# Softmax bias written by the masked score reduction, value halves split out of PSUM, first query stores on GpSimd's queue, and two steps placed later, in a hybrid mLSTM and window-attention layer

## The chip, the core and the metric

The kernel runs on one core of one Trainium2 chip. A core has TensorE (PE, matmuls), VectorE (DVE), ScalarE (ACT), GpSimd (POOL) and SyncE (SP, which here only issues DMAs); each works through its own queue in order, and semaphores tie the queues together. The metric is the device time of one execution in microseconds, and a kernel's time is the median of several runs.

## What is computed

One layer over 4096 tokens of width 1024, all in float32. The rows are normalised, projected to 3856 columns, and the columns feed two groups:

```
scores = (q @ k.T) * 64 ** -0.5                        # 8 query heads, 2 key/value heads, blocks of 128
scores = where(|i - j| <= 128, scores + bias, -1e30)   # T5 relative bias
m      = maximum(max(scores), sink)                    # one learned sink logit per head
p      = exp(scores - m)
out    = (p @ v) / (sum(p) + exp(sink - m))            # group B
h      = mLSTM(q, k, v, gates), forward + backward     # group A, chunks of 128, 4 heads of 128
y      = concat(groupnorm(sigmoid(o) * h) * silu(z_a), out * silu(z_b))
result = rmsnorm(x + y @ w_out)
```

## The kernel before

Four stages follow each other, and TensorE's order is the order of the code (`manual_schedule` for PE). The other engines' orders are made by a scheduler that simulates the program; `behind(c, ins)` tells it not to place an instruction ahead of `ins`, and `high_priority` lets it go ahead of others.

**Stage 1, `pass1` (about 0 to 606 us): window attention.** It runs over 16 blocks of 256 tokens. The fill work is projections with float32 split in two parts, high and low (`kproj`, `vproj`, `qproj`); between its matmuls lie the pieces of attention, four slots per block. A slot is a pair of a 128-token chunk and a key/value head. For slot `sl`, `att_a(sl + 2, g)` makes the scores of query group g = 0 to 3 two slots ahead (L380), adds the bias and reduces a row maximum on VectorE, straight from PSUM (L383, an instruction followed by a short one that reads out the accumulator). The four maxima lie in the tile `st`; after the fourth, L390 forms `NG = min(-max, -sink)` for all four, and four activations (L392) take `exp(s + NG)`. `att_t(sl, i)` transposes 128 columns of four score tiles into a PSUM buffer `tp` of the tag "b", which has two buffers (L412), and ScalarE and VectorE split it into `pt` (L414, L415): the second of these frees the buffer. `att_o(sl - 1, i)` multiplies with the values (L426); ScalarE's copy L438 and VectorE's add L439 empty its result `op` (tag "c", one buffer) into `ab`, which SP stores (L441).

Once per block, `norm_rows(b + 4, LAST["act"])` squares two row tiles on ScalarE (L213, `jk`), behind the latest exponential. `vproj` gathers both halves of a value tile from the PSUM tile `vp` into `vg` in SBUF (L523, L524; 144 columns, 128 of values and 16 of gates), and L527 and L528 split `vg` into `vt`. GpSimd works beside all this on row scaling (L265), splits (L275) and sums (L690 to L693). `sinks()` (L395) closes the stage, and `rnorm` (L798) takes the reciprocal of the row sums `R`, [128, 256], on VectorE (L800).

**Stage 2, `pass2` (about 606 to 1210 us): keys, queries and values of the mLSTM.** It runs over 8 blocks of 512 tokens, from b = 7 down to 0. `qkproj` makes projections, convolution taps (L1053) and SiLU (L1057, L1058) and stores the result to DRAM on SP's queue (L1060). For b = 7 the operands are still in SBUF; the operands `xb` of b = 6 come through SP's queue (L868, eight loads). `ktp` transposes keys into the PSUM tag "b" and splits them (L1101, L1102). `weigh(n)` multiplies a value tile with gate weights (`wvr`, one direction on GpSimd and one on VectorE, L1112) and splits it (L1114, L1115), and `kvmm` multiplies keys with it and carries the state C (L1137), storing kf and C on GpSimd's queue (L1143, L1128). At b = 0 the fill is that of the next stage (L1342).

Stages 3 and 4 (`pass3`, `tail`) scan the chunks and project the output; the change doesn't touch them.

Of the kernel before, what the change touches and what calls it, by code (L numbers as in the profile page):

```python
# [9 lines left out]
F32 = mybir.dt.float32  # L10
F32R = mybir.dt.float32r
BF16 = mybir.dt.bfloat16
AF = mybir.ActivationFunctionType
ALU = mybir.AluOpType
# [10 lines left out]
EV = 400  # L25
# [3 lines left out]
def f32(ap):  # L29
    return ap.bitcast(F32)  # L30
# [85 lines left out]
def behind(c, ins):  # L116
    return c.tc.issue_after(ins.ins) if ins is not None else ExitStack()
# [43 lines left out]
def pass1(c):  # L161
    nc, tc, A = c.nc, c.tc, c.A
    NB = 16
    with ExitStack() as es:
# [168 lines left out]
        bias = []  # L333
# [27 lines left out]
        def att_a(sl, g):  # L361
# [10 lines left out]
            if g == 0:  # L372
                st = wk.tile([128, 4], F32, tag="st", bufs=4, name=f"st{sl}")
                ST[sl] = ([], list(range(jl // 128, jr // 128)), st)
            ps, _, mx = ST[sl]
            ng, rs = c.NG[:, kv, n, :], c.R[:, n, kv, :]
            sp = c.ps("a", [128, 384], f"sp{sl}_{g}")
            qt = qb[kv * 2 + m][:, qc // 64 + half].rearrange("p z q -> p (z q)")
            for z in range(2):
# [4 lines left out]
                                           in1=bias[0][:, kv * 2 + m, lo - 64 * half:hi - 64 * half],  # L384
                                           op0=ALU.add, op1=ALU.max, scale=1.0, scalar=-3e38,
                                           accum_out=mx[:, g:g + 1])
            ps.append(s)
            if g < 3:
                return
            nc.vector.scalar_tensor_tensor(ng, mx, -1.0, nsink[:, kv].rearrange("p h m -> p (h m)"), ALU.mult, ALU.min)  # L390
            for g in range(4):
                LAST["act"] = nc.scalar.activation(ps[g][:, kept(g)], ps[g][:, kept(g)], AF.Exp, bias=ng[:, g:g + 1],  # L392
                                                   accum_out=rs[:, g:g + 1])
# [11 lines left out]
        def att_t(sl, i):  # L405
            ps, js, _ = ST[sl]
            if i >= len(js):
                return
            j = js[i]
            tp = c.ps("b", [128, 512], f"tp{sl}_{j}")  # L410
            for g in range(4):
                nc.tensor.transpose(tp[:, g * 128:(g + 1) * 128], ps[g][:, j * 128:(j + 1) * 128], c.ident)  # L412
            pt = PT[sl, i] = xtile(c, [128, 2, 512], F32R, f"pt{sl}_{j}")
            nc.scalar.copy(pt[:, 0, :], tp)  # L414
            nc.vector.tensor_sub(pt[:, 1, :], tp, f32(pt[:, 0, :]))  # L415
# [90 lines left out]
        def vproj(b):  # L506
            R = {}

            def unit(i, k):
# [12 lines left out]
                with tc.high_priority(offset=EV):  # L522
                    nc.scalar.copy(vg, vp[:, 1, :])  # L523
                    nc.vector.tensor_add(vg, vp[:, 0, :], vg)  # L524
                vt = wk.tile([128, 2, 128], F32R, tag="v", bufs=7, name=f"v{n}")
                vv = vg[:, 0:128].rearrange("p (a d) -> p a d", a=2)
                nc.scalar.copy(vt[:, :, 0:64], vv)  # L527
                nc.vector.tensor_sub(vt[:, :, 64:128], vv, f32(vt[:, :, 0:64]))  # L528
                V[n] = vt
# [153 lines left out]
        fill = qproj(NB - 2) + kproj(NB - 1) + vproj(NB - 1) + qproj(NB - 1) + v2_units(range(31, 27, -1))  # L683
        interleave(fill, pieces)
        sinks()

# [111 lines left out]
def rnorm(c):  # L798
    nc = c.nc
    nc.vector.reciprocal(c.R, c.R)  # L800
    tp = c.ps("b", [128, 2, 128], "rtp")
# [76 lines left out]
def pass2(c):  # L878
    nc, tc, A = c.nc, c.tc, c.A
    with ExitStack() as es:  # L880
# [138 lines left out]
        def qkproj(b, m):  # L1019
# [6 lines left out]
            def unit(lo, hi, k, j):  # L1026
# [28 lines left out]
                def finish():  # L1055
# [3 lines left out]
                    dst = c.k_d if m >= 4 else c.q_d  # L1059
                    nc.sync.dma_start(dst[4 * b:4 * b + 4, :, h * 128:h * 128 + 128].rearrange("n p t -> p n t"),  # L1060
                                      acc.rearrange("p (n t) -> p n t", n=4))
# [83 lines left out]
        for b in range(7, -1, -1):  # L1145
# [40 lines left out]
            def kvp(n, hh):  # L1186
                if hh == 0 and n > n3 - 3:
                    weigh(n - 1)
                kvmm(n, hh)
# [735 lines left out]
```

## Time and profile before

| what | us |
|---|---|
| three runs | 2173.66, 2176.89, 2175.59 |
| median | 2175.59 |
| the profiled execution, its own time | 2170.39 |
| its span, first to last instruction | 2168.7 |
| TensorE busy | 2116.4 |
| VectorE, ScalarE, GpSimd busy | 1547.1, 1132.2, 704.2 |

The profile is of one execution. Its groups give, for a line of the code, the engine, the operation, the output and input tiles, the number of instructions, busy time and mean duration, and the idle time in front of them with what ended it. The table of waits adds such idle time up by who waited for whom: total, number of waits, longest. The timeline lists instructions by start and duration. A TensorE that is busy nearly all the time makes its idle stretches the part that other engines can give back.

### The profile page before, as it was taken

The numbers are of one execution on the slowest core, as the hardware profiler recorded it, in microseconds if no ns is written. First come the engines' busy times: TensorE is split into PE (matmuls) and PEld (weight loads), VectorE is DVE, ScalarE is ACT, GpSimd is POOL, SyncE is SP. The second block draws the span as 40 slices with busy tenths as digits, with TensorE's granted clock in tenths as the row PEclk, the third lists the DMA queues.
The fourth block names the chain that finished last, engine by engine and source line by source line (L and its number), as shares of the span: only waits on it lengthen the run. The fifth ranks groups of instructions, "written<-read, shape, count | busy, mean of one in ns | idle before, by whom it ended". The sixth has DMA issues, their size and how long they took to land. (4 is left out here: it accounts for less than half of the span.)

```text
span 2168.7 us, 35317 instructions
## 1 busy us (share of the span) xinstructions
PE 2116.4 (98%) x12034; PEld 1834.4 (85%) x12034; DVE 1547.1 (71%) x3259; ACT 1132.2 (52%) x2764; POOL 704.2 (32%) x1049
## 2 busy tenths in 40 slices
PE   8999999999999999999999999999999999999998
PEld 7999999999887887888887888888888788888886
DVE  6777777878876786667566777777777443777776
ACT  7778777778654444444433455555555321323323
POOL 3575666653014234322310322223222111112222
PEclk9999999999999999999999999999999999999999
DMA  8563544433228556743676988888888998667775
GB/s 269 181 208 135 194 142 187 161 139 113 64 91 263 188 170 217 246 159 112 216 223 239 340 272 273 254 265 278 268 273 290 353 359 279 181 178 187 192 196 144
DMA packets 286432, 460.71 MB, mean 212 GB/s; under 512 B 23851, under 2 KB 151851, under 8 KB 284716
## 3 DMA queue, kind: packets, MB, share of 16 engines
q1 hardware_dynamic: 246880, 323.94, 46.5%
q0 software_dynamic: 39136, 134.25, 19.0%
q8 instruction: 95, 1.56, 0.3%
q14 instruction: 85, 0.70, 0.1%
q10 hardware_dynamic: 236, 0.27, 0.0%
HBM read 305.20 MB, written 153.17 MB: 211 GB/s over the span
## 5 line engine op out<-in xcount | busy, mean ns | idle before, releaser
L1342 PE MATMUL P<-wt,op 128*128 128x512 f32 x1344 | 360.4, 406 | 0.4 <-DMA op<-xT_d 0.4
L1034 PE MATMUL up<-xb,w 128*128 128x512 f32 x1344 | 335.0, 396 | 0.0
L1691 PE MATMUL o<-wo,yo 128*128 128x512 f32 (+1 forms) x1356 | 311.7, 392 | 0.0
L1691 PEld LDWEIGHTS o<-wo,yo 128*128 128x128 f32 x1356 | 253.2, 188 | 58.6
L1034 PEld LDWEIGHTS up<-xb,w 128*128 128x128 f32 x1344 | 245.1, 188 | 49.1
L1342 PEld LDWEIGHTS P<-wt,op 128*128 128x128 f32 x1344 | 238.5, 189 | 42.5 <-DMA op<-xT_d 0.8
L1053 DVE SCALAR_TENSOR_TENSOR qk<-U,cw,qk 128x512 f32<-128x512 f32 x256 | 194.0, 760 | 85.2 <-ACT qk L1051 81.7
L549 PE MATMUL qp<-xT,wqb 128*128 128x256 f32 x1536 | 241.5, 287 | 0.1
L549 PEld LDWEIGHTS qp<-xT,wqb 128*128 128x128 f32 x1536 | 213.2, 189 | 8.6 <-DVE wqb L320 0.5
L392 ACT ACTIVATE s<-s,NG 128x320 f32<-128x320 f32 (+1 forms) x256 | 140.2, 550 | 46.9 <-DVE NG L390 46.3
L1007 PE MATMUL v2p<-w,xb 128*128 128x512 f32 x672 | 159.1, 396 | 4.7 <-DMA xb<-xT_d 3.1
L1007 PEld LDWEIGHTS v2p<-w,xb 128*128 128x128 f32 x672 | 125.7, 188 | 36.8 <-DMA xb<-xT_d 4.0
L415 DVE TENSOR_TENSOR pt<-tp,pt 128x512 fp32r<-128x512 f32 x188 | 127.9, 687 | 34.1 <-ACT pt L414 32.8
L383 DVE CUSTOM_DVE_ANT_0 s<-sp,G 128x320 f32<-128x320 f32 (+1 forms) x256 | 122.3, 478 | 27.8 <-PE sp L380 25.8
L414 ACT CAST pt<-tp 128x512 fp32r<-128x512 f32 x188 | 108.6, 585 | 52.0 <-PE tp L412 40.3
L412 PE MATMUL tp<-ident,s 128*128 128x128 f32 x752 | 113.5, 273 | 15.9 <-DVE pt L415 15.6
L426 PE MATMUL op<-pt,v 128*128 128x512 f32 x376 | 120.5, 401 | 7.0 <-DVE ab L439 7.0
L380 PE MATMUL sp<-kk,q 128*128 128x320 f32 (+2 forms) x512 | 118.6, 312 | 1.3 <-DVE kk L502 0.8
L1493 ACT ACTIVATE hs<-num,r 128x128 f32<-128x128 f32 x128 | 46.7, 365 | 129.7 <-DVE r L1490 70.9
L151 PE MATMUL zbp<-xc,w 128*128 128x512 f32 x256 | 102.2, 399 | 1.9 <-DVE az L1405 1.4
L412 PEld LDWEIGHTS tp<-ident,s 128*128 128x128 f32 x752 | 85.5, 140 | 20.8 <-issue 17.7
L153 PE MATMUL zbp<-xc,w 128*128 128x512 f32 x256 | 101.0, 395 | 0.0
(307 smaller groups left out, 4543.2 us busy)
## 6 DMA issues: line engine op xcount, KB each, us to landing
xc<-xT_d SPq DMA_DIRECT2D x64, 512.0 KB, 7.3
xT_d<-xT POOLq DMA_DIRECT2D x52, 512.0 KB, 7.3
xb<-xT_d SPq DMA_DIRECT2D x48, 514.0 KB, 7.1
op<-xT_d SPq DMA_DIRECT2D x96, 256.0 KB, 5.5
E<-m_d SPq DMA_DIRECT2D x64, 256.0 KB, 4.3
W<-w_d SPq DMA_DIRECT2D x64, 256.0 KB, 5.9
y<-y_d SPq DMA_DIRECT2D x32, 512.0 KB, 3.4
out<-xr POOLq DMA_DIRECT2D x31, 512.0 KB, 4.4
```

What stands on the lines that cost most here:

```text
L380: nc.tensor.matmul(sp[:, lo:hi], qt, kk[:, kv, z, col - 128 + lo:col - 128 + hi], start=(z == 0), stop=(z == 1))
L383: nc.vector.tensor_tensor_reduce(out=s[:, lo:hi], in0=sp[:, lo:hi], in1=bias[0][:, kv * 2 + m, lo - 64 * half:hi - 64 * half], op0=ALU.add ...
L392: LAST["act"] = nc.scalar.activation(ps[g][:, kept(g)], ps[g][:, kept(g)], AF.Exp, bias=ng[:, g:g + 1], accum_out=rs[:, g:g + 1])
L412: nc.tensor.transpose(tp[:, g * 128:(g + 1) * 128], ps[g][:, j * 128:(j + 1) * 128], c.ident)
L415: nc.vector.tensor_sub(pt[:, 1, :], tp, f32(pt[:, 0, :]))
L426: nc.tensor.matmul(op, vt, pt[:, z, :], start=(i == 0 and z == 0), stop=(i == len(js) - 1 and z == 1))
L549: nc.tensor.matmul(qp, wq[k // 2][:, k % 2, w, m * 128:m * 128 + 128], x[k], start=(k == 0 and j == 0), stop=(k == KT - 1 and j == 2))
L1007: nc.tensor.matmul(vp, a, wv[k // 2][:, k % 2, m, :], start=(k == 0 and j == 0), stop=(k == KT - 1 and j == 2))
L1034: nc.tensor.matmul(up[:, 0:hi - lo], w[k // 2][:, k % 2, a, cs], x, start=(k == 0 and j == 0), stop=(k == KT - 1 and j == 2))
L1053: nc.vector.scalar_tensor_tensor(acc, U[:, t:t + 512], cw[:, cm, t:t + 1], acc, ALU.mult, ALU.add)
L1342: nc.tensor.matmul(P[i], OPS[j, i][:, k, z, :], c.wt[i][k][m], start=k == 0 and a == 0, stop=k == 3 and a == 2)
L1691: nc.tensor.matmul(p, a[:, z, k, :], w[k // 2][:, k % 2, m, lo:hi], start=k == 0 and z == 1, stop=k == 3 and z == 0 and m == 0)
```

## The change

- In `att_a` the reduction L383 now computes `s = -(score + bias)` and `min(s over the row, -sink)`, with `-sink` as an operand per partition, and writes the result straight into the column of `NG`. The tile `st` and the instruction L390 are gone. The exponential takes `scale=-1`.
- In `vproj` the sum of the two halves is made in two instructions, 128 value columns and 16 gate columns. For blocks b > 2 the value part is written back into the PSUM tile `vp`, and the split reads it from there, at high priority.
- `rnorm`'s reciprocal is placed behind the last attention add (`c.abv`).
- In `pass2` the four query stores of the block done first (b = 7) go to GpSimd's queue; the key stores and all other blocks stay on SP's.
- At b = 0 the weighted values of chunks 2, 1 and 0 are placed behind the key splits recorded by then.

```diff
@@ att_a
             if g == 0:
-                st = wk.tile([128, 4], F32, tag="st", bufs=4, name=f"st{sl}")
-                ST[sl] = ([], list(range(jl // 128, jr // 128)), st)
-            ps, _, mx = ST[sl]
+                ST[sl] = ([], list(range(jl // 128, jr // 128)))
+            ps, _ = ST[sl]
...
-                                           op0=ALU.add, op1=ALU.max, scale=1.0, scalar=-3e38,
-                                           accum_out=mx[:, g:g + 1])
+                                           op0=ALU.add, op1=ALU.min, scale=-1.0,
+                                           scalar=nsink[:, kv, half, m:m + 1], accum_out=ng[:, g:g + 1])
...
-            nc.vector.scalar_tensor_tensor(ng, mx, -1.0, nsink[:, kv].rearrange("p h m -> p (h m)"), ALU.mult, ALU.min)
             for g in range(4):
-                LAST["act"] = nc.scalar.activation(ps[g][:, kept(g)], ps[g][:, kept(g)], AF.Exp, bias=ng[:, g:g + 1],
+                LAST["act"] = nc.scalar.activation(ps[g][:, kept(g)], ps[g][:, kept(g)], AF.Exp, scale=-1.0, bias=ng[:, g:g + 1],
                                                    accum_out=rs[:, g:g + 1])
@@ vproj
                     nc.scalar.copy(vg, vp[:, 1, :])
-                    nc.vector.tensor_add(vg, vp[:, 0, :], vg)
+                    for o, cs in ((vp[:, 0, 0:128] if b > 2 else vg[:, 0:128], slice(0, 128)), (vg[:, 128:144], slice(128, 144))):
+                        nc.vector.tensor_add(o, vp[:, 0, cs], vg[:, cs])
...
-                vv = vg[:, 0:128].rearrange("p (a d) -> p a d", a=2)
-                nc.scalar.copy(vt[:, :, 0:64], vv)
-                nc.vector.tensor_sub(vt[:, :, 64:128], vv, f32(vt[:, :, 0:64]))
+                vv = (vp[:, 0, 0:128] if b > 2 else vg[:, 0:128]).rearrange("p (a d) -> p a d", a=2)
+                with tc.high_priority(offset=EV if b > 2 else 0):
+                    nc.scalar.copy(vt[:, :, 0:64], vv)
+                    nc.vector.tensor_sub(vt[:, :, 64:128], vv, f32(vt[:, :, 0:64]))
@@ pass1, rnorm
+        c.abv = LAST["abv"]
         sinks()
...
-    nc.vector.reciprocal(c.R, c.R)
+    with behind(c, c.abv):
+        nc.vector.reciprocal(c.R, c.R)
@@ qkproj
-                    nc.sync.dma_start(dst[4 * b:4 * b + 4, :, h * 128:h * 128 + 128].rearrange("n p t -> p n t"),
+                    q = nc.gpsimd if b == 7 and m < 4 else nc.sync
+                    q.dma_start(dst[4 * b:4 * b + 4, :, h * 128:h * 128 + 128].rearrange("n p t -> p n t"),
@@ kvp
                 if hh == 0 and n > n3 - 3:
-                    weigh(n - 1)
+                    with behind(c, None if b else c.kta), behind(c, None if b else c.ktv):
+                        weigh(n - 1)
```

TensorE's order is the same instruction by instruction. On the other engines the order moves; line numbers of the changed kernel differ by a few, so L390 is then the exponential, L412 and L413 the two parts of `pt`, L382 the reduction.

**ScalarE in one block of stage 1.** `s` are score tiles (their exponentials), `jk` the squares, `pt_2` the copy of a slot's last transposed piece, `q` query splits, `ab` the attention result. Before:

```order
L438 COPY ab_1118<-op_1173 64x2x4x64
L414 CAST pt_1_1227<-tp_1_1222 128x512
L392 ACTIVATE s_0_136,R<-s_0_136,NG 128x320
L392 ACTIVATE s_1_137,R<-s_1_137,NG 128x320
L559 ACTIVATE q_1_1284<-qp_1_1219 64x4x64 x2
L392 ACTIVATE s_0_142,R<-s_0_142,NG 128x320
L392 ACTIVATE s_1_143,R<-s_1_143,NG 128x320
L213 ACTIVATE jk_0_1270,ss_1269<-xr_1160 128x1024
L213 ACTIVATE jk_1_1272,ss_1269<-xr_1160 128x1024
L414 CAST pt_2_1262<-tp_2_1257 128x512
L414 CAST pt_0_1320<-tp_0_1315 128x512
```

The same place of the changed kernel:

```order
L390 ACTIVATE s_0_142,R<-s_0_142,NG 128x320
L436 COPY ab_1112<-op_1166 64x2x4x64
L412 CAST pt_1_1220<-tp_1_1215 128x512
L390 ACTIVATE s_1_143,R<-s_1_143,NG 128x320
L213 ACTIVATE jk_0_1262,ss_1261<-xr_1154 128x1024
L213 ACTIVATE jk_1_1264,ss_1261<-xr_1154 128x1024
L559 ACTIVATE q_1_1276<-qp_1_1212 64x4x64 x2
L390 ACTIVATE s_2_138,R<-s_2_138,NG 128x320
L412 CAST pt_2_1254<-tp_2_1249 128x512
L390 ACTIVATE s_3_139,R<-s_3_139,NG 128x320
L412 CAST pt_0_1311<-tp_0_1306 128x512
```

The four exponentials of a slot no longer stand together ahead of the squares: each stands behind its own score, only the last (`s_1_143`) is directly ahead of the squares, and an exponential of the next slot now stands between the squares and `pt_2`.

**VectorE in block 0 of stage 2.** `kt` are key splits, `wvr` and `wvl` weighted values and their low parts, `qk` taps and SiLU of the last key head, `o` an eviction of the next stage, `C` the state. Before:

```order
L1053 SCALAR_TENSOR_TENSOR qk_7_13324<-U_7_13296,cw,qk_7_13324 128x512
L1115 TENSOR_TENSOR wvl_13491<-wvr_13492,wvh_13490 128x1032
L1112 TENSOR_TENSOR wvr_13545<-v_0_13002,TM 128x4x129
L1053 SCALAR_TENSOR_TENSOR qk_7_13324<-U_7_13296,cw,qk_7_13324 128x512
L1058 SCALAR_TENSOR_TENSOR qk_6_13286<-th_6_13330,qk_6_13286 128x512
L1102 TENSOR_TENSOR kt_0_1_13367<-ktp_0_13361,kt_0_0_13366 128x512
L1102 TENSOR_TENSOR kt_1_1_13387<-ktp_1_13381,kt_1_0_13386 128x512
L1053 SCALAR_TENSOR_TENSOR qk_7_13324<-U_7_13296,cw,qk_7_13324 128x512
L1115 TENSOR_TENSOR wvl_13544<-wvr_13545,wvh_13543 128x1032
```

The same place of the changed kernel:

```order
L1105 TENSOR_TENSOR kt_0_1_13271<-ktp_0_13265,kt_0_0_13270 128x512
L1055 SCALAR_TENSOR_TENSOR qk_7_13228<-U_7_13200,cw,qk_7_13228 128x512 x2
L1105 TENSOR_TENSOR kt_1_1_13291<-ktp_1_13285,kt_1_0_13290 128x512
L1327 TENSOR_TENSOR o_13306<-P_1_13280,o_13278 128x512
L1060 SCALAR_TENSOR_TENSOR qk_7_13228<-th_7_13295,qk_7_13228 128x512
L1105 TENSOR_TENSOR kt_2_1_13319<-ktp_2_13313,kt_2_0_13318 128x512
L1115 TENSOR_TENSOR wvr_13330<-v_2_12844,TM 128x4x129
L1140 SCALAR_TENSOR_TENSOR C_13336<-C_12716,decay,kv_0_13338 128x129
L1329 TENSOR_TENSOR z_13346<-P_2_13308,o_13306 128x512
L1118 TENSOR_TENSOR wvl_13329<-wvr_13330,wvh_13328 128x1032
L1140 SCALAR_TENSOR_TENSOR C_13336<-C_12716,decay,kv_1_13350 128x129
L1105 TENSOR_TENSOR kt_3_1_13363<-ktp_3_13357,kt_3_0_13362 128x512
```

The key splits `kt_0` to `kt_2` now stand ahead of all three late weighted values, and the low part of chunk 2's stands ahead of `kt_3`.

**SP's queue at the end of the first block of stage 2.** `k_d` and `q_d` are key and query stores, `xb` the operands of the next block. Before:

```order
L1060 DMA k_d<-qk_6_8279 128x4x128
L1060 DMA k_d<-qk_7_8397 128x4x128
L1060 DMA q_d<-qk_0_8484 128x4x128
L868 DMA xb_0_8664<-xT_d 128x2x514
L868 DMA xb_1_8666<-xT_d 128x2x514
```

The same place of the changed kernel:

```order
L1063 DMA k_d<-qk_6_8183 128x4x128
L1063 DMA k_d<-qk_7_8301 128x4x128
L870 DMA xb_0_8568<-xT_d 128x2x514
L870 DMA xb_1_8570<-xT_d 128x2x514
L870 DMA xb_2_8572<-xT_d 128x2x514
```

The first query store no longer stands ahead of the loads. On GpSimd's queue it now stands between the first store of kf and the store of C that follows it; the second stands behind the last store of C, ahead of two small memsets; the third and the fourth among the transfers of the next block's side work.

More of the change, by code (lines that the diff above doesn't have):

```diff
@@ L405, in att_t @@
         def att_t(sl, i):
-            ps, js, _ = ST[sl]
+            ps, js = ST[sl]
             if i >= len(js):
```

## The prediction

> **What bounds the kernel.** I read the page's first part, then the table of waits of TensorE, then windows of the stages, then the timelines around each wait. First the page's busy times, and the head of the waits (waiter, releaser, total us, times, longest):
>
> ```profile
> span 2168.7 us, 35317 instructions
> PE 2116.4 (98%) x12034; PEld 1834.4 (85%) x12034; DVE 1547.1 (71%) x3259; ACT 1132.2 (52%) x2764; POOL 704.2 (32%) x1049
> ```
> ```profile
> PE tp L412 <- DVE pt L415: 15.6, 13, 1.8
> PE op L426 <- DVE ab L439: 7.0, 6, 2.4
> PE bps L337 <- POOL ohb L300: 6.5, 1, 6.5
> PE v2p L1007 <- DMA xb<-xT_d: 3.1, 2, 2.1
> PE ktp L1099 <- DVE kt L1102: 2.8, 2, 1.5
> ```
>
> TensorE is busy for 2116.4 of 2168.7 us, and the change leaves its instructions and their order alone. So only its 52.3 us of idle time can be won. The change aims at four of these five rows (28.5 us); the one-hot wait L300 (6.5) stays. Most of the first row lies in the loop of stage 1. The window of ten blocks (length, then busy us of PE, weight load, DVE, ACT, POOL; clock; DMA share), and on TensorE two of the waits in it:
>
> ```profile
> 110.00:463.00 353.00, 338.72 (x2562) 326.10 (x2561) 273.49 (x691) 272.44 (x725) 220.87 (x281) 1.00 0.46 166
> ```
> ```profile
> 132.25 0.63 PE L412 MATMUL tp<-ident,s 128*128 128x128 f32 x4 [1.84 <-DVE pt L415]
> ...
> 165.51 0.64 PE L549 MATMUL qp<-xT,wqb 128*128 128x256 f32 x4
> 167.52 0.63 PE L412 MATMUL tp<-ident,s 128*128 128x128 f32 x4 [1.38 <-DVE pt L415]
> ```
>
> The granted clock is 1.00. The window holds 353.00 − 338.72 = 14.28 us of idle PE, about 1.4 in each 35.3 us block, and the table has 13 such waits. VectorE is busy 27.3 us of a block, so no engine but PE is full: it is an order that costs the 1.4 us. ScalarE and VectorE at the wait of 167.52:
>
> ```profile
> 160.88 0.56 ACT L392 ACTIVATE s<-s,NG 128x320 f32<-128x320 f32 x1 [2.22 <-DVE NG L390]
> ...
> 161.98 0.75 ACT L559 ACTIVATE q<-qp 64x256 fp32r<-64x256 f32 x2
> ...
> 163.32 0.55 ACT L392 ACTIVATE s<-s,NG 128x320 f32<-128x320 f32 x1
> 163.87 1.04 ACT L213 ACTIVATE jk<-xr 128x1024 bf16<-128x1024 f32 x1
> ...
> 166.07 1.07 ACT L414 CAST pt<-tp 128x512 fp32r<-128x512 f32 x2
> ```
> ```profile
> 159.21 0.08 DVE L383 DVE_READ_ACCUMULATOR2_ANT st<- 128x1 f32 x1
> 159.21 0.69 DVE L415 TENSOR_TENSOR pt<-tp,pt 128x512 fp32r<-128x512 f32 x1
> 159.82 1.02 DVE L390 SCALAR_TENSOR_TENSOR NG<-st,nsink 128x4 f32<-128x4 f32 x1
> ```
> ```profile
> 159.50 1.31 POOL L693 TENSOR_TENSOR xraw<-xraw 128x512 f32<-128x512 f32 x1
> ```
>
> PE wants its buffer at 165.51 + 0.64 = 166.15. ScalarE begins the copy `pt_2` that frees it only at 166.07: four exponentials and two squares stand ahead, and ScalarE had idled 2.22 us for L390. L390 itself, of [128, 4], waited behind a `pt` part and then took 1.02 us; it ends at 160.84, beside the end of GpSimd's L693 at 160.81. The groups of VectorE in this window (count | busy us, mean ns), and L390 by itself over the kernel (min/median/max ns):
>
> ```profile
> L383 DVE CUSTOM_DVE_ANT_0 s<-sp,G 128x320 f32<-128x320 f32 x160 | 77.5, 484 | 11.8 <-PE sp L380 10.6
> L390 DVE SCALAR_TENSOR_TENSOR NG<-st,nsink 128x4 f32<-128x4 f32 x40 | 31.4, 785 | 0.7
> L528 DVE TENSOR_TENSOR v<-vg,v 128x128 fp32r<-128x128 f32 x20 | 13.8, 692 | 0.0
> L524 DVE TENSOR_TENSOR vg<-vp,vg 128x144 f32<-128x144 f32 x20 | 5.9, 297 | 0.0
> ```
> ```profile
> L390 DVE SCALAR_TENSOR_TENSOR NG<-st,nsink x64: 143/164/1839, 39.6 to 592.8; 128x4 f32<-128x4 f32 x64
> ```
>
> L390 needs 143 ns and takes 785 on average in the loop. L390 and L528 have two SBUF inputs; L524, larger than L528 but with one input in PSUM, takes 297 ns. **The Trainium skill**, page "SBUF — State Buffer", section "🔬 SBUF: two separate sides", has this as an exclusive lock between a VectorE operation with two SBUF inputs and a GpSimd operation that reads SBUF. The rows agree.
>
> **The softmax part.** L383 already reads scores and bias; the minimum and the sign are other operations of the same instruction, so 484 ns stay. The accumulator's readout now writes `NG`. Gone are 40 × 785 ns = 31.4 us of VectorE. `scale=-1` is an argument of an instruction that stays. More important is when the exponentials may start: each behind its own score. In the block above the last score's readout ends at 159.29. ScalarE, idle there, has done three exponentials by then. The walk, with 163.87 − 163.32 = 0.55 us per exponential: the last one 159.35 to 159.9, two squares (166.07 − 163.87 = 2.20) to 162.1, `q_1` 0.75 to 162.85, the next slot's first exponential to 163.4, the `pt_2` copy (half of 1.07, say 0.6) to 164.0, VectorE's part 0.69 to 164.7. PE wants it at 166.15: 1.45 us to spare, and the next thing late is PE's own work. So I take the loop's 14.3 us whole. The rest of the waits for L415 (15.6 − 14.3 = 1.3 us) has the same chain in shorter blocks; I take 1.0.
>
> **The value halves.** In the loop 20 additions are split into 128 + 16 columns; the extra instruction costs between 0.08 (the readout above) and 0.30 us (L524): 1.6 to 6 us in 353 us of a VectorE that has 79.5 to spare and loses 31.4. Split L528 loses an SBUF input: from 692 ns towards L524's 297, 20 × 0.4 = 7.9 us less. VectorE's load becomes 273.5 − 31.4 − 7.9 + 3 = 237, 23.7 us per block. The PSUM buffer of `vp` is now held until the split is done, about a copy and a subtraction (0.6 + 0.69) longer. Its tag has three buffers and no wait of PE for it stands among the five rows, so I price that at 0. Without cover it would be 20 × 1.3 = 26 us; a gain is excluded, as no wait is there to lose.
>
> **The waits for `ab`** (7.0 in six). The longest, and what VectorE and ScalarE did:
>
> ```profile
> 600.37 0.73 PE L426 MATMUL op<-pt,v 128*128 128x512 f32 x2 [2.37 <-DVE ab L439]
> ```
> ```profile
> 597.85 1.74 DVE L800 RECIPROCAL R<-R 128x256 f32<-128x256 f32 x1
> 599.62 0.69 DVE L439 TENSOR_TENSOR ab<-op,ab 64x512 f32<-64x512 f32 x1
> ...
> 614.57 3.18 DVE L1053 SCALAR_TENSOR_TENSOR qk<-U,cw,qk 128x512 f32<-128x512 f32 x4 [5.10 <-ACT qk L1051]
> ```
> ```profile
> 597.34 0.58 ACT L438 COPY ab<-op 64x512 f32<-64x512 f32 x1 [0.34 <-PE op L426]
> ```
>
> ScalarE's copy ends at 597.92, and the reciprocal stands in front of the addition until 599.59. Behind the last addition, it falls into an idle stretch of 5.1 us. The addition then runs 597.92 to 598.61, and PE, free at 600.37 − 2.37 = 598.00, still waits 0.6: 1.75 us won. The other five (7.0 − 2.37 = 4.63 us) stand behind other VectorE and ScalarE work. Between 0 and 4.6 I take 2.0, since less work stands ahead but part of it waits for a store.
>
> **The query stores.** PE waits 3.1 us for `xb` (the table's fourth row). SP's queue, and the DMA share (last but one column) shortly before and during the loads:
>
> ```profile
> 637.67 3.37 SPq L1060 DMA_DIRECT2D k_d<-qk  x2
> 652.13 0.36 SPq L1060 DMA_DIRECT2D q_d<-qk  x1
> 652.72 7.88 SPq L868 DMA_DIRECT2D xb<-xT_d  x8
> ```
> ```profile
> 645.00:650.00 5.00, 5.00 (x43) 5.00 (x43) 5.00 (x9) 2.43 (x6) 1.35 (x2) 1.00 0.00 2
> 660.00:665.00 5.00, 5.00 (x42) 4.80 (x40) 0.26 (x2) 1.11 (x6) 0.86 (x2) 1.00 1.04 371
> ```
>
> SP waits 11 us (641.0 to 652.1) for a query tile, with the loads behind it and the DMA engines at 0.00. Moved to GpSimd's queue, the store lets at least the first loads go while the engines are free. On GpSimd the first store has only that block's C store behind it, whose data comes no earlier. Between 0 and 3.1 I take 2.5.
>
> **The weighted values at b = 0.** PE's two waits and VectorE ahead of them:
>
> ```profile
> 1193.54 0.63 PE L1099 MATMUL ktp<-ident,qk 128*128 128x128 f32 x4 [1.51 <-DVE kt L1102]
> 1198.50 0.65 PE L1099 MATMUL ktp<-ident,qk 128*128 128x128 f32 x4 [1.29 <-DVE kt L1102]
> ```
> ```profile
> 1189.70 1.22 DVE L1115 TENSOR_TENSOR wvl<-wvr,wvh 128x1032 fp32r<-128x1032 f32 x1
> 1190.85 0.68 DVE L1112 TENSOR_TENSOR wvr<-v,TM 128x516 f32<-128x516 f32 x1
> ```
>
> A weighted value costs VectorE 0.68 + 1.22 = 1.9 us; without one ahead, a split can come 1.9 us earlier, more than either wait. But the low part of chunk 2 then stands ahead of `kt_3`: up to 1.22 us, partly covered; I charge 0.8. Between a loss of 1.2 and a gain of 2.8 I take 2.8 − 0.8 = 2.0.
>
> **The sum.** 14.3 + 1.0 + 1.75 + 2.0 + 2.5 + 2.0 = 23.55, less 1.5 for new small waits (an allowance of about one more wait like the loop's 1.38): 22.0. The profiled execution, 2170.4 by its own time, would be 2148.4. It lay 5.2 below the median of 2175.6, so the median goes to 2175.6 − 22.0 = 2153.6.
>
> **Rivals.**
>
> *The squares still hold `pt_2`* (0.10). If the last exponential starts no earlier because its score, not L390, is late in most blocks, the loop stays and only 22.0 − 14.3 = 7.7 is won: 2167.9. For it: the squares still stand ahead. Against: the 2.22 us of idle ScalarE.
>
> *The new operand brings L390's stretching into the reduction* (0.05). If the per-partition `-sink` made L383 share with GpSimd as L390 does, each of 16 reductions per block would gain 785 − 143 = 642 ns: 10.3 us, and VectorE 23.7 + 10.3 = 34.0 of the 35.3 − 1.4 = 33.9 us that PE needs. The loop's gain would mostly go; at a loss of 6 the time is 2159.6. The Trainium skill's section named above puts the lock on two SBUF inputs and does not say whether such an operand counts. Against it, an operation with a state in SBUF, an input in PSUM and a per-partition decay keeps its length, 120 times, in a stage in which GpSimd works too:
>
> ```profile
> L1137 DVE SCALAR_TENSOR_TENSOR C<-C,decay,kv x120: 332/343/353, 653.6 to 1208.4; 128x129 f32<-128x129 f32 x120
> ```
>
> *The loads of `xb` end no earlier* (0.08). At 1.04 the DMA engines are full while they load, so an earlier issue may not end earlier; then 2.5 is lost: 2156.1. By the Trainium skill, "DMA: Bandwidth & Descriptors", section "Issuing engines are not separate DMA queues", all queues share the same 16 engines and another issuer saves only issue time, which speaks for this. But the share of 0.00 at 645 to 650 shows that here the queue's order kept them idle.
>
> *Slower: exponentials between the copies* (0.07). ScalarE's exponentials now stand one by one among the `pt` and `ab` copies, each bound to its own score. If once per slot a copy that PE waits for stands behind an exponential that waits for its reduction, 0.48 + 0.55 = 1.03 us, 40 slots of the loop lose 41 us against 22: 2194.6. It decides from 22 / 40 = 0.55 us per slot. For it: ScalarE is busy 272 of 353 us. Against: where I walked it, 1.45 us are to spare and the scores are ready first.
>
> *No effect* (0.04). If the exponentials still wait until all four columns of the `NG` tile are written and the other waits only change names: 2175.
>
> **The numbers.** The forecast, 2153.6, has 0.66. Low: all of 15.6 + (7.0 − 0.6) + 3.1 + 2.8 = 27.9 gives 2147.7, less 1.9 by which the fastest run lies below the median: about 2146. High: the first rival, 2168. Outside lie the slower case, no effect, and the tails. A measurement tells about 0.2%, 4.4 us, from no change: faster 0.66 + 0.10 + 0.05 + 0.08 = 0.89, same 0.04, slower 0.07.
>
> **What would show it.** Right: in the window of ten blocks PE idles under 2 us and the tp row falls below 2; ScalarE's wait for L390 is gone and the last exponential starts within 0.2 us of its readout; L383 keeps 484 ns; the reciprocal starts after 608; the first `xb` issue comes before 645; no wait of `ktp` over 0.8. Wrong: waits of PE for `pt` with an exponential directly ahead of the copy, L383 above 0.7 us, or new waits for `vp`.

## The result and the profile after

| | kernel before, us | changed kernel, us | ratio, 95% interval |
|---|---|---|---|
| first set (4 and 4 runs) | 2176.24 | 2162.18 | 0.9939, 0.9922 to 0.9957 |
| second set (11 and 6 runs) | 2171.89 | 2156.27 | 0.9929, 0.9914 to 0.9944 |

Faster by 14 to 16 us. The forecast was 22 us (2153.6, a ratio of 0.990), so the direction and the range held, and the gain was about two thirds of the one forecast. First the changed kernel's busy times, then TensorE's largest waits apart from the one-hot wait at the start:

```profile
span 2160.7 us, 35339 instructions
PE 2120.3 (98%) x12034; PEld 1837.9 (85%) x12034; DVE 1519.9 (70%) x3227; ACT 1140.9 (53%) x2764; POOL 709.8 (33%) x1053
```
```profile
PE op L424 <- DVE ab L437: 8.1, 8, 3.0
...
PE kv L151 <- DVE C L1140: 2.9, 2, 2.1
PE P L1346 <- DMA op<-xT_d: 1.9, 1, 1.9
PE xtp L460 <- DVE kk L500: 1.7, 1, 1.7
```

The span fell by 8.0 us (2168.7 to 2160.7) between the two profiled executions. TensorE's idle time fell by 11.9 (52.3 to 40.4), but the same 12034 matmuls took 3.9 us longer (2116.4 to 2120.3). Three of the rows of before that the change aimed at are gone: `tp` (15.6), `xb` (3.1) and `ktp` (2.8). The `ab` row grew from 7.0 to 8.1, and the last three rows above are new or larger.

This pair shows only 8.0 of the 14 to 16 us. The profiled execution of before (2170.4) lies under the lowest of that kernel's timed runs (2173.7), and its granted clock was 0.999 in the mean; the changed kernel's was 2162.4, near its median, at 0.997. A second profile of the changed kernel has a span of 2153.1 us:

```profile
PE 2116.7 (98%) x12034; PEld 1836.5 (85%) x12034; DVE 1519.1 (71%) x3227; ACT 1140.5 (53%) x2764; POOL 706.0 (33%) x1053
```

There TensorE is idle for 36.4 us, 15.9 less than in the profile of before, and its busy time is that of before. So what comes back as waits and as a lower clock differs from one execution to the next.

The window of ten blocks of stage 1, and in it ScalarE and VectorE at the place that the prediction walked through:

```profile
110.00:463.00 353.00, 349.98 (x2645) 337.11 (x2644) 261.10 (x698) 287.04 (x752) 232.26 (x299) 1.00 0.58 176
```
```profile
160.39 0.56 ACT L390 ACTIVATE s<-s,NG 128x320 f32<-128x320 f32 x1 [0.74 <-DVE NG L382]
...
160.95 1.04 ACT L213 ACTIVATE jk<-xr 128x1024 bf16<-128x1024 f32 x1
...
163.81 0.56 ACT L390 ACTIVATE s<-s,NG 128x320 f32<-128x320 f32 x1
...
164.49 0.59 ACT L412 CAST pt<-tp 128x512 fp32r<-128x512 f32 x1
```
```profile
160.27 0.08 DVE L382 DVE_READ_ACCUMULATOR2_ANT NG<- 128x1 f32 x1
```

TensorE now idles 3.0 us here instead of 14.28, and no wait for `pt` is left among it; the waits that are left are for `ab`. The last score's readout ends at 160.35 and its exponential starts at 160.39. From there to the `pt_2` copy it is 164.49 − 160.39 = 4.1 us, as walked (159.35 to 163.4, 4.05).

The reciprocal stands behind the last addition, where the prediction put it (at 595.98 and not after 608, since the stage ends some 12 us earlier). The addition of `ab` no longer has it ahead, and what is left of that wait is 0.70 us (0.6 was forecast):

```profile
587.80 0.74 PE L424 MATMUL op<-pt,v 128*128 128x512 f32 x2 [0.70 <-DVE ab L437]
```
```profile
595.25 0.69 DVE L437 TENSOR_TENSOR ab<-op,ab 64x512 f32<-64x512 f32 x1
595.98 1.75 DVE L802 RECIPROCAL R<-R 128x256 f32<-128x256 f32 x1
```

**Where the missing part went.** At 80 us TensorE waits for `ab`, because ScalarE's copy into the single `ab` buffer waits for the store of the chunk before. The window behind it shows the granted clock (third number from the right):

```profile
82.83 0.73 PE L424 MATMUL op<-pt,v 128*128 128x512 f32 x2 [2.95 <-DVE ab L437]
```
```profile
81.48 0.58 ACT L436 COPY ab<-op 64x512 f32<-64x512 f32 x1 [3.70 <-DMA at_d<-ab]
```
```profile
78.00:84.00 6.00, 3.05 (x23) 2.75 (x23) 2.38 (x9) 2.49 (x7) 5.24 (x9) 0.98 0.87 201
84.00:88.00 4.00, 4.00 (x21) 3.90 (x21) 1.61 (x8) 1.70 (x7) 0.65 (x4) 0.61 0.94 244
645.00:649.00 4.00, 2.51 (x21) 2.30 (x20) 1.23 (x1) 1.73 (x5) 0.54 (x1) 1.00 1.05 363
650.00:654.00 4.00, 4.00 (x23) 4.00 (x22) 1.05 (x4) 0.54 (x2) 0.54 (x1) 0.57 1.04 356
```

The second pair of windows belongs to the moved query stores. The `xb` loads now start at 637.45 and fill the DMA engines (1.05). Most of the 15 us between 637.45 and the 652.72 of before is the earlier end of stage 1. Measured from the end of the key stores, the loads start 9.0 us behind (628.46, then 637.45) instead of 11.7 (641.04, then 652.72). They do not start at once, as the prediction had it, because, by the profile, the loads then wait for the instructions that last used their buffers (from 626 to 640 us: total, times, longest):

```profile
SPq L870 <- PE up L1036: 4.9, 2, 4.6
SPq L870 <- DVE wvl L1118: 4.3, 1, 4.3
```

Then the stores of kf and C are late: VectorE waits for the store of C, and TensorE for VectorE. (ScalarE's wait for the store of kf, last line, comes behind that of TensorE.)

```profile
637.45 11.43 SPq L870 DMA_DIRECT2D xb<-xT_d  x8
```
```profile
649.60 0.36 PE L151 MATMUL kv<-wvh,kt 128*128 128x258 f32 x1 [2.08 <-DVE C L1140]
```
```profile
649.10 1.25 DVE L1140 SCALAR_TENSOR_TENSOR C<-C,decay,kv 128x129 f32<-128x129 f32 x4 [0.61 <-DMA cb_d<-C]
```
```profile
651.13 0.27 ACT L1138 COPY kf<-kv 128x129 f32<-128x129 f32 x1 [3.40 <-DMA kf_d<-kf]
```

Which transfer holds the store of C is not settled. On GpSimd's queue it now stands directly behind the first query store:

```profile
639.82 0.78 POOL L1063 DMA_DIRECT2D q_d<-qk  x1 [0.60 <-DVE C L1140]
640.59 0.54 POOL L1131 DMA_DIRECT2D cb_d<-C  x1
```

VectorE could go on at 649.10, 8.5 us after that issue. Without the moved stores (below) the same store is issued at 639.15 and VectorE goes on at 645.51, 6.4 us later, with the loads beside it too. No run separates the earlier loads from the query store that now stands ahead.

Behind each of the two waits of TensorE (2.95 and 2.08 us) it ran some 4 us at a mean clock of about 0.6. At 0.61 and 0.57 a stretch of 4 us loses about 1.6 us, so the two lose some 3.3 of the 3.9 us by which TensorE's busy time grew. This is an estimate: in three profiles without such a stretch (before, and two of the kernels below) the same 12034 matmuls take between 2114.3 and 2116.9 us. In the medians the clock counts for less than in this pair: in the second set it was 0.9979 in the mean of the runs before and 0.9973 in those of the changed kernel, by estimate about 1 us.

### The profile page after: what moved, and what is told of

The parts are those of the page before. It is cut to its first block, busy times and chain, and to the rows that moved or that the text cites. A ratio compares the mean times of both kernels' runs of the same rounds, so it can differ in the third digit from the quotient of the medians.

```text
span 2160.7 us, 35339 instructions
## 1 busy us (share of the span) xinstructions
PE 2120.3 (98%) x12034; PEld 1837.9 (85%) x12034; DVE 1519.9 (70%) x3227; ACT 1140.9 (53%) x2764; POOL 709.8 (33%) x1053
## 5 line engine op out<-in xcount | busy, mean ns | idle before, releaser
L413 DVE TENSOR_TENSOR pt<-tp,pt 128x512 fp32r<-128x512 f32 x188 | 129.7, 690 | 83.2 <-ACT pt L412 79.9
L390 ACT ACTIVATE s<-s,NG 128x320 f32<-128x320 f32 (+1 forms) x256 | 142.4, 557 | 51.5 <-DVE NG L382 49.8
L382 DVE CUSTOM_DVE_ANT_0 s<-sp,G,nsink 128x320 f32<-128x320 f32 (+1 forms) x256 | 138.1, 539 | 37.9 <-PE sp L379 33.7
L412 ACT CAST pt<-tp 128x512 fp32r<-128x512 f32 x188 | 109.9, 584 | 44.0 <-PE tp L410 18.6
L151 PE MATMUL zbp<-xc,w 128*128 128x512 f32 x256 | 102.1, 399 | 2.8 <-DVE az L1409 1.4
L153 PE MATMUL zbp<-xc,w 128*128 128x512 f32 x256 | 101.0, 394 | 0.0
L152 PE MATMUL zbp<-xc,w 128*128 128x512 f32 x256 | 100.9, 394 | 0.0
```

Of the source, the lines that this page charges most:

```text
L382: nc.vector.tensor_tensor_reduce(out=s[:, lo:hi], in0=sp[:, lo:hi], in1=bias[0][:, kv * 2 + m, lo - 64 * half:hi - 64 * half], op0=ALU.add ...
```

## The experiments

Each kernel ran beside the kernel before on the same chip. Ratios are to that kernel, with their 95% intervals. The kernel before took 2171.4 to 2171.9 us in these sets and 2176.2 in the first, so 4 to 5 us are to be taken off where an expectation names a time.

| kernel | median us | before us | ratio, interval |
|---|---|---|---|
| changed kernel without the softmax part | 2172.64 | 2171.43 | 1.0002, 0.9992 to 1.0011 |
| without the value halves | 2157.40 | 2171.43 | 0.9936, 0.9920 to 0.9952 |
| without the moved stores | 2154.56 | 2171.43 | 0.9914, 0.9902 to 0.9927 |
| without the late weighted values | 2155.14 | 2171.43 | 0.9922, 0.9910 to 0.9935 |
| the changed kernel, second set | 2156.27 | 2171.89 | 0.9929, 0.9914 to 0.9944 |
| a copy releases four exponentials | 2154.80 | 2171.89 | 0.9924, 0.9909 to 0.9938 |
| constant in place of −sink | 2159.35 | 2171.89 | 0.9941, 0.9927 to 0.9956 |
| two `ab` buffers | 2160.65 | 2171.89 | 0.9945, 0.9930 to 0.9961 |
| kernel before with the softmax part alone | 2159.56 | 2171.72 | 0.9944, 0.9931 to 0.9957 |
| copy, stores on SP | 2154.40 | 2171.72 | 0.9924, 0.9907 to 0.9941 |
| copy, stores on SP, weighted values early | 2153.98 | 2171.72 | 0.9925, 0.9912 to 0.9938 |

**The softmax part undone.** `st`, the maximum and the step L390 are back.

```diff
-                                           op0=ALU.add, op1=ALU.min, scale=-1.0,
-                                           scalar=nsink[:, kv, half, m:m + 1], accum_out=ng[:, g:g + 1])
+                                           op0=ALU.add, op1=ALU.max, scale=1.0, scalar=-3e38,
+                                           accum_out=mx[:, g:g + 1])
...
+            nc.vector.scalar_tensor_tensor(ng, mx, -1.0, nsink[:, kv].rearrange("p h m -> p (h m)"), ALU.mult, ALU.min)
```

> The changed kernel with only the softmax part undone: the tile of maxima and the step that forms all four biases are back. My theory: this part alone brought the gain of the loop of stage 1, so TensorE's idle time there goes from 3.0 back to 12 to 14 us and the time from 2162.2 to about 2173. Rival: the other parts carry a good half of the gain, and the time stays under 2168.

The window of ten blocks, the wait, and L390's group in that window (count | busy us, mean ns):

```profile
110.00:463.00 353.00, 335.75 (x2539) 323.40 (x2539) 268.53 (x706) 269.23 (x716) 218.02 (x278) 1.00 0.45 163
```
```profile
PE tp L412 <- DVE pt L415: 19.0, 12, 1.8
```
```profile
L390 DVE SCALAR_TENSOR_TENSOR NG<-st,nsink 128x4 f32<-128x4 f32 x39 | 32.6, 837 | 0.6
```

The other four parts together give 1.0002: nothing that can be measured. The loop idles 17.3 us (353.00 − 335.75), more than before the change, and L390 is as long as ever. The zero hides two effects: in this profiled execution TensorE idles 49.3 us in all (2166.2 − 2116.9), so 32.0 outside the loop instead of 38.0. So in the profile the other parts win 6.0 us there and the loop takes 3.0 of them back; the medians show nothing of the rest.

**The value halves undone.**

```diff
-                    for o, cs in ((vp[:, 0, 0:128] if b > 2 else vg[:, 0:128], slice(0, 128)), (vg[:, 128:144], slice(128, 144))):
-                        nc.vector.tensor_add(o, vp[:, 0, cs], vg[:, cs])
+                    nc.vector.tensor_add(vg, vp[:, 0, :], vg)
...
-                vv = (vp[:, 0, 0:128] if b > 2 else vg[:, 0:128]).rearrange("p (a d) -> p a d", a=2)
+                vv = vg[:, 0:128].rearrange("p (a d) -> p a d", a=2)
```

> Only the value halves undone: one addition of 144 columns, the split reads SBUF again. My theory: VectorE's groups for it get longer (the split from about 0.3 to about 0.7 us), but TensorE doesn't wait for them, and the time is 2162 within 1.5. Rival: the split, stretched beside GpSimd, delays the halves of the transposed scores, and the time is over 2165.

The split's group on VectorE, first in this kernel, then in the changed one:

```profile
L527 DVE TENSOR_TENSOR v<-vg,v 128x128 fp32r<-128x128 f32 x22 | 24.3, 1104 | 0.7 <-ACT v L526 0.7
```
```profile
L528 DVE TENSOR_TENSOR v<-vp,v 128x128 fp32r<-128x128 f32 x22 | 6.2, 283 | 0.5 <-ACT v L527 0.5
```

The same subtraction takes 1104 ns on average with two SBUF inputs (286 to 2221) and 283 with one of them in PSUM (270 to 292): 18 us of VectorE in the window. The time stays within the interval of the changed kernel; no row of TensorE's waits names the split.

**The query stores undone.**

```diff
-                    q = nc.gpsimd if b == 7 and m < 4 else nc.sync
+                    q = nc.sync
```

> Only the query stores undone: all on SP's queue. My theory: what the earlier loads win (3.1 us of waits) they give back as the new wait for the stores of C and kf (2.1) and the 4 us at a clock of 0.58 behind it (about 1.7), so the time is 2162 within 1.5 and the clock behind that stage stays 1.00. Rival: the early loads are a clean gain, and the time is over 2164.5. A third: they cost more than they win, under 2160.

SP's queue and TensorE's wait:

```profile
638.62 0.36 SPq L1063 DMA_DIRECT2D q_d<-qk  x1
639.21 6.87 SPq L870 DMA_DIRECT2D xb<-xT_d  x8
```
```profile
PE v2p L1009 <- DMA xb<-xT_d: 2.2, 2, 2.0
```

The loads start at 639.21, so the prediction's sign, a first issue before 645, would have come true without this part. The wait for the loads is back with 2.2 us; the one at 649 for the store of C is gone, and no clock under 0.97 lies behind this stage. At 0.9914 this is the best ratio measured, on another chip than the changed kernel's 0.9929, and the intervals overlap. The time, 2154.56, is 2.9 us under the 2157.4 that "2162" means in this set, which is between my theory and its third case. So the moved stores are no measurable gain; that they cost is suggested, not shown.

**The late weighted values undone.**

```diff
-                    with behind(c, None if b else c.kta), behind(c, None if b else c.ktv):
-                        weigh(n - 1)
+                    weigh(n - 1)
```

> Only the late weighted values at block 0 undone. My theory: the two waits of the key transposes (2.8 us) come back, and of the waits of 0.84 (kv) and 1.90 (operands of the next stage) that the changed kernel has there at least the first goes: time 2162 to 2164. Rival: the wait for the next stage's operands only moved there, since that stage starts earlier, and stays near 1.9; then the time is about 2164.

```profile
PE ktp L1102 <- DVE kt L1105: 2.8, 2, 1.5
```

The key waits are back (2.8). The waits there for C (0.84) and for the operands of the next stage (1.90, in the second profile of the changed kernel 0.6) shrink to 0.34 in all; no difference in time. This kernel's profile shows something else. Its wait at 80 us is the same 2.95 us as in the changed kernel, and the windows are:

```profile
78.00:84.00 6.00, 3.05 (x24) 2.76 (x21) 2.38 (x8) 2.67 (x8) 4.25 (x9) 1.00 0.66 211
84.00:88.00 4.00, 4.00 (x34) 3.91 (x33) 2.59 (x9) 2.68 (x9) 0.64 (x4) 1.00 1.03 352
```

The clock stays at 1.00. So the same wait can throw the clock down in one execution and not in another.

**The changed kernel again.**

> The changed kernel again, unchanged, with more rounds and beside the three that follow. My theory: its ratio to before is the 0.994 measured first, since each execution has one or two stretches of 4 us at a clock near 0.5. Rival: that was an unlucky set, and the ratio is 0.991 to 0.992, like two of the kernels with one part undone.

0.9929, between the two values that the expectation names. Its profile has one stretch of low clock (82 to 86 us, clock 0.50 to 0.65), the first set's had two. Over its six runs the mean clock goes from 0.998 (2153.61) to 0.996 (2162.03).

**The exponentials released together.** The reduction writes to `st`, and ScalarE copies it:

```diff
-                                           scalar=nsink[:, kv, half, m:m + 1], accum_out=ng[:, g:g + 1])
+                                           scalar=nsink[:, kv, half, m:m + 1], accum_out=mx[:, g:g + 1])
...
+            nc.scalar.copy(ng, mx)
             for g in range(4):
```

> The changed kernel, but the four columns of a slot's bias come from the reduction into a small tile and a ScalarE copy of 4 columns forms NG, so that all four exponentials wait for the fourth score, as before the change, while VectorE has no step of two SBUF inputs. If the gain of the loop comes from the exponentials starting one by one (my theory in the prediction), the waits for pt come back with 0.5 to 1 us a block and the time is 5 to 10 us above the changed kernel. If it comes from L390 no longer being stretched beside GpSimd (rival), TensorE's idle time in the loop stays under 5 us and the time is within 3 us of the changed kernel.

The window, ScalarE at the same place as above, and TensorE's waits for `pt` and `ab`:

```profile
110.00:463.00 353.00, 351.24 (x2659) 338.28 (x2658) 260.80 (x699) 288.86 (x794) 232.04 (x295) 1.00 0.49 173
```
```profile
157.23 0.20 ACT L390 COPY NG<-st 128x4 f32<-128x4 f32 x1 [0.74 <-DVE st L383]
157.46 0.56 ACT L392 ACTIVATE s<-s,NG 128x320 f32<-128x320 f32 x1
...
162.65 1.08 ACT L414 CAST pt<-tp 128x512 fp32r<-128x512 f32 x2
```
```profile
PE tp L412 <- DVE pt L415: 4.4, 6, 1.8
PE op L426 <- DVE ab L439: 2.8, 5, 1.3
```

All four exponentials wait for the fourth score and stand ahead of the squares, as before the change. Yet the loop idles only 1.8 us, and the time is that of the changed kernel. From the first exponential to `pt_2` it is 5.2 us, as before the change (160.88 to 166.07). What is gone is the late start: 0.26 us after the readout (157.20) instead of 1.6 (159.29 to 160.88). My theory falls and the rival holds in its main point: the gain of the loop is the removal of L390, not the release one by one. The release decides which small waits are left: here 4.4 us for `pt`, of which the changed kernel has none, and 2.8 for `ab` instead of its 8.1.

The rival said more, that L390 was stretched beside GpSimd. The mean of 785 ns hides how. A block has four L390, and in the kernel before they look like this (the third, 1.02 us at 159.82, is the one of the prediction):

```profile
143.34 1.79 DVE L390 SCALAR_TENSOR_TENSOR NG<-st,nsink 128x4 f32<-128x4 f32 x1
150.58 0.16 DVE L390 SCALAR_TENSOR_TENSOR NG<-st,nsink 128x4 f32<-128x4 f32 x1
170.87 0.16 DVE L390 SCALAR_TENSOR_TENSOR NG<-st,nsink 128x4 f32<-128x4 f32 x1
```

The two long ones run beside instructions of GpSimd (L275 from 143.29, L693 from 159.50 to 160.81). Of the short ones, the first comes within the last 0.2 us of such an instruction, and the second has none beside it. Each of the ten blocks has two long and two short ones. TensorE's wait for `pt` follows only the third; no wait of TensorE follows the longest. Of the third's late start of 1.6 us, about 0.86 is the stretch (1.02 − 0.16), and most of the rest is its place behind a `pt` part on VectorE. The copy removed both, and no run separates them.

**A constant in place of −sink.** The sink is left out of the maximum that is subtracted.

```diff
-                                           scalar=nsink[:, kv, half, m:m + 1], accum_out=ng[:, g:g + 1])
+                                           scalar=3e38, accum_out=ng[:, g:g + 1])
```

> The changed kernel with a constant instead of the per-partition -sink in the reduction: the sink is left out of the maximum that is subtracted. If the operand per partition is what lengthened the reduction from 484 to about 540 ns, it goes back to 484; if the minimum and the sign did it, it stays at 540. Either way 256 x 0.055 = 14 us of VectorE are mostly off the path: I expect the time within 2 us of the changed kernel. Rival: they delay ab behind the reductions, and the time falls by 3 us or more.

The reduction's group in the window of ten blocks, first in the changed kernel, then here:

```profile
L382 DVE CUSTOM_DVE_ANT_0 s<-sp,G,nsink 128x320 f32<-128x320 f32 x166 | 90.6, 546 | 27.6 <-PE sp L379 24.2 <-PE tp L410 2.4
```
```profile
L382 DVE CUSTOM_DVE_ANT_0 s<-sp,G 128x320 f32<-128x320 f32 x167 | 81.3, 487 | 20.6 <-PE sp L379 18.7
```

The operand per partition costs 59 ns an instruction; the minimum and the sign cost nothing (484 before). The time doesn't fall. This profile has three stretches of low clock (behind waits of 2.7, 2.2 and 3.8 us).

**Two `ab` buffers.**

```diff
-                AB[n] = wk.tile([128, 4, 128], F32, tag="ab", bufs=1, name=f"ab{n}")
+                AB[n] = wk.tile([128, 4, 128], F32, tag="ab", bufs=2, name=f"ab{n}")
...
-                vg = wk.tile([128, 144], F32, tag="vg", bufs=2, name=f"vg{n}")
+                vg = wk.tile([128, 144], F32, tag="vg", bufs=1, name=f"vg{n}")
```

> The changed kernel with two buffers for ab instead of one (paid for with one buffer for vg). My theory: the wait of 2.95 us at 80 us, in which ScalarE's copy into ab waits for the store of the chunk before, goes, and with it the 4 us at half clock that mostly follow it: 3 to 5 us faster than the changed kernel. Rival: the wait has another cause behind it (the addition's place on VectorE), and less than 1 us is won.

The wait at 80 us is gone, so it hung on the single buffer. But the 3 to 5 us that I expected did not come. The order shifted elsewhere, and a wait as long came at 24.7 us, with a low clock behind it (last windows row):

```profile
27.63 1.08 PE L460 MATMUL xtp<-ident,x 128*128 128x128 f32 x4 [2.94 <-DVE q L563]
```
```profile
28.00:32.00 4.00, 4.00 (x27) 4.00 (x26) 1.07 (x4) 1.40 (x4) 0.79 (x4) 0.70 1.10 270
```

What the buffer alone is worth stays open, since it had to be paid for with another.

**The softmax part alone**, on the kernel before (the first diff reversed).

> The kernel before with the softmax part alone. My theory: this part is the whole gain and the other four net to nothing, so the ratio to before is 0.992 to 0.994, with TensorE's idle time in the loop under 4 us; the reciprocal's wait (2.4 us), the wait for the xb loads (3 us) and the two key waits (2.8 us) stay. Rival: the value halves are needed with it (the split with two SBUF inputs then holds the pt parts), and the ratio is over 0.995.

```profile
110.00:463.00 353.00, 349.88 (x2642) 336.94 (x2643) 273.15 (x675) 286.51 (x751) 232.19 (x298) 1.00 0.57 176
```
```profile
PE ktp L1097 <- DVE kt L1100: 2.8, 2, 1.5
```

0.9944, 12 of the 14 to 16 us, a little less than I expected; the loop idles 3.1 us without the value halves, which it doesn't need. VectorE is as busy in the window (273.15 us) as before the change (273.49), so the gain is not a matter of VectorE's load. Of the waits that I expected to stay, only the two for the keys do. The wait for `xb` is 1.2 instead of 3.1, and the reciprocal's is gone although nothing holds it back here: the scheduler put it at 583.80, away from the addition, and TensorE waits 0.78 us instead of 2.37:

```profile
583.80 1.74 DVE L798 RECIPROCAL R<-R 128x256 f32<-128x256 f32 x1
...
588.22 0.73 PE L424 MATMUL op<-pt,v 128*128 128x512 f32 x2 [0.78 <-DVE ab L437]
```

**Two combinations** of the copy with undone parts.

> The changed kernel with the ScalarE copy that releases the four exponentials together, and all query stores on SP's queue. My theory: the waits of the scattered exponentials (1.65 at 44, 2.3 to 3 at 80, 0.9 at 450 us) are gone as in the kernel with the copy alone, and so is the wait for the store of C; with fewer waits over 2 us there are fewer stretches at half clock. Ratio to before 0.990 to 0.992, the best so far. Rival: it's within noise of the changed kernel, 0.993.

> As the kernel before this one, with the late weighted values undone too. The two key waits come back (2.8 us) and the waits of 0.8 (kv) and up to 1.9 (operands of the next stage) go: within 1.5 us of it either way.

Neither can be told from the changed kernel, and the rival of the first holds. Its six runs of one program lie between 2149.13 us at a mean clock of 0.999 and 2161.67 at 0.996; a clock lower by 0.003 is about 6.5 us (an estimate), so half of that spread. The profiled one is the slowest, with three stretches of low clock and not the fewer that I expected; the last, behind a wait of 2.23 us for `w` in stage 3, looks so:

```profile
1660.00:1664.00 4.00, 3.92 (x15) 3.35 (x15) 2.78 (x9) 1.35 (x8) 1.03 (x1) 0.57 0.46 107
```

## Why the prediction was right in direction and half again too large

- **What bounds the kernel** was right: only TensorE's idle gaps could be won, and the loop's were the main part. The softmax part is the only one whose absence is seen in the time (1.0002 without it).
- **"More important is when the exponentials may start: each behind its own score"** was the wrong half of that step. The copy kernel keeps them together and wins the same. What had to go was a step at the head of a chain with about 1.4 us too little time: it ended 1.6 us after the score that it needed. The row that said so stood in the prediction: the 2.22 us that ScalarE waited for L390. So the loop's term came out for a reason that the prediction gave second place.
- **The loop's idle time** was taken "whole", 14.3 us. Its waits for `pt` did go whole, but 3.0 us came back there as waits for `ab`, so the loop gave 11.3. The sign "under 2 us" was missed here (3.0) and met in the second profile of the changed kernel (1.8).
- **The removed waits** were sized well: `tp` 15.6 (forecast 15.3), `xb` 3.1 (2.5), `ktp` 2.8 (2.0) and the reciprocal 2.37 − 0.70 = 1.67 (1.75). That the reciprocal's size fits is luck: with the softmax part alone that wait is 0.78 us, so placing the reciprocal is not shown to be what removed it. The `xb` wait went with the loads 2.7 us earlier against the key stores, not the 11 us of the walk. The 2.0 for the other waits for `ab` was wrong in sign: without the reciprocal's 2.37 they were 4.6, and with what is left of it set aside they are now 7.4 (8.1 − 0.7). Less load on VectorE did nothing for them; with the exponentials scattered, the wait at 80 us for the single buffer's store came to the front. With the exponentials together the whole row is 2.8 (and 4.4 stand in the row of `pt`).
- **The step that failed is the allowance of 1.5 us for new waits.** In the profiled pair the four rows fell by 20.4 us (15.6 + 3.1 + 2.8 − 1.1), and 8.5 came back (20.4 − 11.9): 2.9 for C, 1.5 for the next stage's operands, 1.8 at the transposes of x and 0.9 for `w`, 7.1 in all, and smaller ones. In the second profile of the changed kernel the four rows fell by 22.4 and 6.5 came back. For the query stores the prediction looked only at the store of C behind the moved one, "whose data comes no earlier", and not at what holds that store up once it is issued. The kernel without the moved stores has none of the wait at 649.
- **A term was missing: the clock.** I read 1.00 in the loop of before and gave the clock no term. TensorE's busy time grew by 3.9 us in the profiled pair; between the medians of the second set the clock is worth about 1 us, by the estimate above.
- **The rivals and signs.** The operand's lengthening was real but 59 ns and not 642, and it is nearly the same in every instruction of the window (529 to 554 ns), in which GpSimd comes and goes, so it is not the stretching of L390; "L383 keeps 484 ns" was wrong, "above 0.7 us" did not come: 16 × 59 ns are 0.9 us in a block in which VectorE is idle for about 9 (353 − 261 us over some ten blocks). No new wait for `vp` came, and none for the key transposes over 0.8 us. "The squares still hold `pt_2`" did not happen. "Slower" showed only as the small waits for `ab`. "The loads of `xb` end no earlier" did not come true: the wait for them (3.1 us) is gone, but a wait for the store of C on the other queue came. The Trainium skill ("DMA: Bandwidth & Descriptors", section "Issuing engines are not separate DMA queues") says that transfers of all queues interleave on the same 16 engines. The trace does not contradict it: the engines' share is 1.05 from 645 to 649, and the store of C on GpSimd's queue held VectorE until 8.5 us after its issue. Whether the loads or the query store ahead of it did that is open, as said.

## What to carry to other kernels

A tiny step at the head of a chain can be the whole bound: look for an instruction whose mean is several times its minimum, see which of its executions the waits follow, and remove it or move it to an engine that is free there. Shortening such an instruction is worth nothing where nothing waits for it: the split of the values lost 18 us of VectorE time and won no time. A gain that is read off a table of waits is an upper end; on this kernel, 98% busy, about a third of it came back, as waits elsewhere and as a lower clock. Compare several executions before explaining what is missing, since one pair of profiles can show half the gain. And check what a transfer that is issued earlier will run beside.

## What the runs showed of the hardware

- **The granted clock can fall to 0.5 behind a wait of TensorE of some 1.7 us or more, but need not.** Such stretches last 3 to 4 us. They followed waits of 2.95 and 2.08 us (the changed kernel), 2.52 (without the moved stores), 2.34 (the changed kernel again), 2.03 and 2.23 us (copy, stores on SP), 2.94 and 1.65 us (two `ab` buffers), 2.72, 2.20 and 3.77 us (constant in place of −sink) and 1.76 us (the copy). None followed waits of 2.95 us (without the weighted values), 2.37 and 2.10 (before, at 598 and 677 us), 2.03 (without the moved stores, at 662 us) and 2.19 us (copy, stores on SP, at 738 us), nor the ten waits of 1.3 to 1.8 us in the loop of before. In three executions one followed some 2 us of matmuls with a single row and a wait of only 0.28. The Trainium skill, "TensorE: Matmul & The Clock Gate", section "🔬 Part 1: The HAM clock gate (the "warmup" mystery)", tells of a free-running window of about 3.4 us in which activity is watched, and lets the clock go down after at least one idle window. Here shorter waits were enough at times, and the measurement decides. That it depends on where a wait falls in such a window would fit these runs, but no run here shows the window.
- **A subtraction of [128, 128] on VectorE takes 1104 ns on average with two SBUF inputs (286 at the least) and 283 with one in PSUM**, in a loop in which GpSimd is busy for 232 of 353 us.
- **An operand per partition adds 59 ns** to a masked reduction of [128, 320] (487 to 546).
